# Projections by float32 matmuls on the two column halves of TensorE in place of three float32r passes

## The chip, the cores and the metric

The kernel runs on one core of a Trainium2 chip. The metric is the device time of one execution in microseconds (us). The runs shown are three, from 2896.31 to 2898.53 us with a median of 2897.43.

## The reference

The reference is one step of a two-layer streaming encoder with 1024 model features, for a prompt of 1024 frames and a group of 8 x 16 sample frames, 1152 frames in all. Everything is float32. Cut to its trunk:

```python
for i in range(DEPTH):                       # 2 layers
    a = _rms(h, norm_mix_pre[i])
    if i < N_A_LAYERS:                       # layer 0: forgetting attention, 16 heads x 64
        proj = a @ fox_w_in[i]               # q, k, v and the log-forget column
        ...
        mix = o.reshape(b, t, FOX_HEADS * HEAD_DIM) @ fox_w_out[i]
    else:                                    # layer 1: sliding window, 16 query and 4 key heads
        q = (a @ swa_w_q[j]).reshape(b, t, SWA_Q_HEADS, HEAD_DIM)
        o = swa_attend(q, kv_k, kv_v, swa_sinks[j])
        mix = o.reshape(b, t, SWA_Q_HEADS * HEAD_DIM) @ swa_w_out[j]
    h = h + _rms(mix, norm_mix_post[i])
    f = _swiglu(_rms(h, norm_ffn_pre[i]), ffn_w_gate[i], ffn_w_up[i], ffn_w_down[i])   # D_FF = 2816
    h = h + _rms(f, norm_ffn_post[i])
    gate = jax.nn.sigmoid(_rms(h, ple_norm[i]) @ ple_w_gate[i] + ple_b_gate[i])
    h = h + gate * (p[i] @ ple_w_proj[i])
    if i == N_A_LAYERS - 1:
        kv = (_rms(h, kv_norm) @ swa_w_kv).reshape(b, t, 2, SWA_KV_HEADS, HEAD_DIM)
```

The products written with `@` are the projections of the title. The attentions' own products (scores, weights times values) are not among them.

## The kernel before

Activations lie with features on the 128 partitions, in three chunks of C = 384 frames. A projection's weights are cut into blocks of 128 x 128; one output tile of 128 features by 384 frames collects eight such blocks (KT = 8) in one PSUM buffer, and ScalarE or VectorE takes it out.

**Parts.** Projections run in the matmul type float32r. Every operand of a projection is made into two tiles: a high part, `round_r` (line 139, a ScalarE copy into a float32r tile), and a low part, `low_part` (line 145, on VectorE: operand minus high part). The helper `mm3` (lines 215 to 217) then issues three float32r matmuls into the same PSUM tile: high weights by high activations, high by low, low by high. The value projections have the same three matmuls written out, with the activations as the stationary operand: `v_tile` of layer 0 (lines 578 to 580, 272 or 384 columns) and `v_tile` in `kv_steps` (lines 1859 to 1861, 256 columns).

**Where parts come from.** `Weights` loads raw weights (tile wraw), scales them where a norm's gain is folded in, and makes the tiles whi and wlo (`round`, `low`). Weights with the mark "parts" were split earlier: `presplit` loads a quarter of a unit, scales it, rounds it (line 1499), subtracts (line 1502), and stores both parts to wpg_d or wkq_d, in the shade of the channel mixer; `Weights.round` later loads both parts. Activations are split by `plan_split` (ahi, alo), `o_high`/`o_low`, `operand` (four high and four low slices of one tile), `c_high`/`c_low`, `p0_high`/`p0_low` and `ple_parts`.

**The channel mixer.** For two of the three chunks the gate, up and down projections use Strassen's scheme (seven products for a 2 x 2 cut of the weights and the chunks); the third chunk is multiplied plainly. `matrix` handles one pair of weight units of gate or up: sums of weights (`s_sum`, line 1314), their parts (`parts_of`), `product` (four mm3 into banks X, Y, Z) and `plain`. Results go to rows (tag row, 10 buffers) and to t_d and hc_d in device memory. The down projection is a loop of `kstep`: load one row of activations (`h_load`), split it (`h_high`, `h_low`), split the slice of weights (`w_high`, `w_low`), then 4 or 8 mm3 into PSUM tiles pd. `strassen` forms weight differences for it in two buffers of tag sq (`temp_diff`, line 1627) or in place (line 1632).

**Order.** In the first stage and in `layer_tail` the order of the instructions on each engine is made by `Plan`: each step is added with an engine, a cost in us, the steps it follows, the buffers it takes and frees and a due time; `run` simulates the four queues (PE, ACT, DVE, LOAD, the last being the load queue on SP) and emits the steps in the order found. `tile_steps` adds one projection tile in two or more pieces, `serpentine` runs a projection over the three chunks, turning round so that weights at the turn are used again. The two attentions are emitted in program order, with `Pipe` deciding when delayed work (transposes, values) comes in. In the second one `queries` (16 tiles in pieces of three, three and two blocks) and `embed` (24 tiles) are put between score rows by `fill`.

**float32 matmuls already there.** The attentions' values are such: `fox_values` (line 1007) and `swa_values` (line 2046) multiply, for two heads e = 0 and 1, 64 columns of values each, and write the two halves of the partitions of one PSUM tile, tile pV:

```python
for e in range(2):
    nc.tensor.matmul(pv[0][e * HD:(e + 1) * HD, q0:256], vp[:, j, e * HD:(e + 1) * HD],
                     PT[e][j // 4][:, j % 4, q0:], start=j == 0, stop=j == nj - 1)
```

So is the cumulative sum over frames (line 762, 16 columns of weights). Sums over features for the norms (`total`, line 233, three matmuls) and their spreading (`spread`, line 254, three transposes) are full-width PE work between the projection tiles.

Of the kernel before, what the change touches and what calls it, by code (L numbers as in the profile page):

```python
# [20 lines left out]
KT = 8  # L21
# [67 lines left out]
def tile_kernel(ctx: ExitStack, tc: tile.TileContext, i, o, upto=99):  # L89
# [53 lines left out]

    def low_part(out, x, hi):
        return nc.vector.tensor_tensor(out, x, hi.bitcast(F32), SUB)  # L145

    class Weights:
# [21 lines left out]
        def round(self, k):  # L169
            src, gain = self.specs[k]  # L170
            if gain == "parts":
                t = self.sets[k % len(self.sets)]
                hl = [wp.tile([P, 1024], F32R, name="w" + x, tag=f"w{x}{t}") for x in ("hi", "lo")]
                for x in range(2):
                    nc.sync.dma_start(hl[x].bitcast(F32), src[:, x])
                self.done[k] = hl
                return
# [8 lines left out]
            lo = wp.tile([P, 1024], F32R, name="wlo", tag=f"wlo{t}")  # L186
            self.done[k] = hi, lo
            return round_r(self.eng, hi[:, :n], raw[:, :n])

        def low(self, k):  # L190
            if k in self.raws:
                n = self.specs[k][0].shape[-1]
                hi, lo = self.done[k]
                return low_part(lo[:, :n], self.raws.pop(k)[:, :n], hi[:, :n])
# [17 lines left out]
    def mm3(ps, w, a, first, last, more=False):  # L212


        nc.tensor.matmul(ps, w[0], a[0], start=first, stop=False, skip_group_check=more)  # L215
        nc.tensor.matmul(ps, w[0], a[1], start=False, stop=False, skip_group_check=more)  # L216
        nc.tensor.matmul(ps, w[1], a[0], start=False, stop=last, skip_group_check=more)  # L217
# [111 lines left out]
    def plan_unit(plan, W, k, due=1e9, needs=()):  # L329
# [7 lines left out]
        if W.specs[k][1] == "parts":  # L337
            plan.turn[part] = [plan.add(LOAD, 2.9, step(W.load, k), turn(part), takes=[part])]
            return plan.turn[part][0]
# [8 lines left out]
        return plan.add(DVE, 0.07 + 0.00104 * n, step(W.low, k), [r], frees=["raw"])  # L348
# [42 lines left out]
    def plan_split(plan, src, after, put, free=(), read=()):  # L391
# [4 lines left out]
        def high(k):  # L396
            if not out:
                out.extend((act_slot(F32R, "ahi"), act_slot(F32R, "alo")))
                put(tuple(out))
            round_r("a", out[0][:, k, :], src()[:, k, :])  # L400

        def low(k):
            low_part(out[1][:, k, :], src()[:, k, :], out[0][:, k, :])

        for k in range(KT):
            x = plan.add(ACT, 0.42, step(high, k), [after[k]] + first, takes=[] if first else ["act", "act"])
            first = first or [x]
            done.append(plan.add(DVE, 0.47, step(low, k), [x] + done[-1:]))
        if free:
            plan.add(DVE, 0.0, lambda: None, done + list(read), frees=list(free))  # L410
# [49 lines left out]
    def w_out(l):  # L460
# [5 lines left out]
        keep(W.low(0))  # L466
        return W

    def out_parts(c, ks):
# [3 lines left out]
        def split(k):  # L473
            if not parts:
                parts.extend((act_slot(F32R, "ohi"), act_slot(F32R, "olo")))
            keep(round_r("a", parts[0][:, k, :], oc[c][:, k, :]))
            keep(low_part(parts[1][:, k, :], oc[c][:, k, :], parts[0][:, k, :]))
# [47 lines left out]
    def ple_parts(praw, c, part):  # L525

        pa = []
        for k in range(2):
            hi, lo = part(0), part(1)
            with tc.high_priority(offset=HP):  # L530
                round_r("a", hi, praw[:, c, k])
                low_part(lo, praw[:, c, k], hi)
# [36 lines left out]
    def v_tile(piece, blk, ps=None, ks=range(KT)):  # L569
# [5 lines left out]
        for k in ks:  # L575
            hi, lo = Wv.get(4 * piece + k // 2)
            ws = slice((k % 2) * n, (k % 2 + 1) * n)
            nc.tensor.matmul(ps[:, :n], ahi[:, k, ts], hi[:, ws], start=k == 0, stop=False)
            nc.tensor.matmul(ps[:, :n], ahi[:, k, ts], lo[:, ws], start=False, stop=False)
            nc.tensor.matmul(ps[:, :n], alo[:, k, ts], hi[:, ws], start=False, stop=k == KT - 1)  # L580
# [34 lines left out]
    def p0_high(c, k):  # L615
        hi, lo = (tp.tile([P, C], F32R, name="phl", tag=f"phl{x}", bufs=4) for x in range(2))
        round_r("a", hi, praw[:, c, k])
        pa.setdefault(c, []).append((hi, lo))

    def p0_low(c, k):  # L620
        low_part(pa[c][k][1], praw[:, c, k], pa[c][k][0])
# [16 lines left out]
    def wp_step(k, h, part):  # L638
# [6 lines left out]
        elif part == 1:  # L645
            if h == 0:
                Wp.done[k] = [wp.tile([P, 1024], F32R, name="w" + x, tag=f"w{x}{k}") for x in ("hi", "lo")]
            round_r("a", Wp.done[k][0][:, cs], Wp.raws[k][:, cs])
        else:
            low_part(Wp.done[k][1][:, cs], Wp.raws[k][:, cs], Wp.done[k][0][:, cs])  # L650
# [17 lines left out]
    for h in range(2):  # L668
        for k in range(2):
# [3 lines left out]
            wlow[h].append(plan.add(DVE, 0.6, step(wp_step, k, h, 2), [x], frees=["raw"] if h else []))  # L673
# [5 lines left out]

    def p0(c):  # L680
        split = []
        for k in range(2):
            x = plan.add(ACT, 0.42, step(p0_high, c, k), [px[c]], takes=["phl"])
            split.append(plan.add(DVE, 0.47, step(p0_low, c, k), [x], frees=["act"] if c == 2 and k else []))
        for f in range(KT):
            end = f == KT - 1
            x = plan.tile(0.985, step(p0_tile, c, f), split + wlow[f // 4], takes=["mm"],
                          frees=(["phl", "phl"] + (["w0", "w1"] if c == 2 else [])) if end else [])
            x = plan.add(ACT, 0.37, step(p0_out, c, f), [x], takes=["ev"] if c == 2 else [], frees=["mm"], due=plan.clock + EVAC)
# [12 lines left out]

    def v0(c):
# [4 lines left out]
        for blk in range(3 * c, 3 * c + 3):  # L708
            x = plan.tile(1.41, step(v0_tile, blk, 0), na[c][:4] + wv[:2], takes=["mm"])
            x = plan.tile(1.41, step(v0_tile, blk, 1), na[c][4:] + wv[2:] + [x], frees=["w0", "w1"] * 2 if blk == 8 else [])  # L710
# [353 lines left out]
    def layer_tail(l, oc, Wo, oa0, order, specs_kv=(), more=None):  # L1064
# [56 lines left out]
        def tile_steps(key, unit, act, needs_w, needs_a, frees=(), pieces=2):  # L1121
# [7 lines left out]
            for p in range(pieces):  # L1129
                x = plan.tile(4.17 / pieces, step(piece, p * n, n), [x] + needs_a[p * n:(p + 1) * n], takes=["mm"] if p == 0 else [],  # L1130
# [3 lines left out]
        def serpentine(W, at, order, act, needs, then, free):  # L1134
# [4 lines left out]
            last = {at[n][f]: (n, f) for n, f in seq}  # L1139
            for j, (n, f) in enumerate(seq):  # L1140
# [3 lines left out]
                               frees + (free if j % KT == KT - 1 else []), 2 if j % KT else NPC)  # L1144
# [3 lines left out]
        def o_high(c, k):  # L1148
            if oa[c] is None:
                oa[c] = act_slot(F32R, "ohi"), act_slot(F32R, "olo")  # L1150
            round_r("a", oa[c][0][:, k, :], oc[c][:, k, :])

        def o_low(c, k):
            low_part(oa[c][1][:, k, :], oc[c][:, k, :], oa[c][0][:, k, :])
# [3 lines left out]
        for c in order:  # L1158
            split, first = [], [None] * (c == cC)
            for k in range(KT):  # L1160
# [5 lines left out]
                split.append(plan.add(DVE, 0.47, step(o_low, c, k), [x] + split[-1:], frees=["act"] if k == KT - 1 else []))  # L1166
# [41 lines left out]
        def operand(name, c, k0, after=()):  # L1208

            def high(j):  # L1210
                if j == 0:
                    acts[name] = act_slot(F32R, name)
                round_r("a", acts[name][:, j], mix[c][:, k0 + j])

            def low(j):
                low_part(acts[name][:, 4 + j], mix[c][:, k0 + j], acts[name][:, j])

            for j in range(4):
# [3 lines left out]
                add(DVE, 0.47, step(low, j), r=[("m", c, k0 + j), (name, 0, j)], w=[(name, 1, j)])  # L1222
# [9 lines left out]
        def c_high(k):  # L1232
            if k == 0:
                cp_[:] = act_slot(F32R, "chi"), act_slot(F32R, "clo")
            round_r("a", cp_[0][:, k], mix[cC][:, k])

        def c_low(k):
            low_part(cp_[1][:, k], mix[cC][:, k], cp_[0][:, k])

        first = []  # L1240
        for k in range(KT):
            x = add(ACT, 0.42, step(c_high, k), r=[("m", cC, k)], w=[("chi", k)], after=first, takes=[] if k else ["act", "act"])
            first = first or [x]
            add(DVE, 0.47, step(c_low, k), r=[("m", cC, k), ("chi", k)], w=[("clo", k)])
# [15 lines left out]
        nC = [wrote["clo", k] for k in range(KT)]  # L1260
# [11 lines left out]
        def parts_of(m, u, src, skey):  # L1272
# [4 lines left out]
            def high():  # L1277
                units_[m, u] = [wp.tile([P, 1024], F32R, name="w" + x, tag=f"w{x}{t}") for x in ("hi", "lo")]
                round_r("a", units_[m, u][0], src())

            def low():
# [989 lines left out]
```

## Time and profile before

| what | value |
|---|---|
| median of three runs | 2897.43 us |
| the profiled execution | 2892.37 us, span 2890.6 us |
| TensorE (PE), matmuls | busy 2845.3 us, 98%, 17612 records |
| weight loads (PEld) | busy 2733.4 us, 95% |
| VectorE (DVE) | busy 1843.8 us, 64% |
| ScalarE (ACT) | busy 1259.9 us, 44% |
| GpSimd (POOL) | busy 198.3 us, 7% |
| data moved by DMA | 440.29 MB |

The stages by the lines at work: first projections to about 150 us, query and key projection of layer 0 to about 350, forgetting attention to 608, the tail of layer 0 (output projection, channel mixer, embedding gate, then the next layer's keys, values and first queries) to 1685, sliding-window attention to 1898, the tail of layer 1 to the end.

How to read a row of the groups: line, engine, operation, output<-input by tile names, then for matmuls rows*columns of the weights and partitions x elements of the moving operand, the number of records, busy time in us, mean ns of one, and the engine's idle time before them with what ended it. Both float32r and float32 are shown as f32. Matmul records overlap in a pipeline, so a mean is a latency. A row of the stretches gives for each engine busy us and records in brackets, then the granted clock of PE as a share of full speed, the DMA share and GB/s.

### The profile page before, as it was taken

The page shows a single profiled execution, that of the slowest core. Times are in us where ns is not written, and L with a number is a line of the kernel's source. Part 1 is how long each engine was busy: PE and PEld are TensorE (multiplying, and loading weights), DVE is VectorE, ACT ScalarE, POOL GpSimd, SP SyncE. Part 2 cuts the span into 40 slices and gives each one's busy share as a digit, 9 for nine tenths or more (in the row PEclk, how much of TensorE's full clock was granted, in tenths as well). Part 3 has the DMA queues.
Part 4 walks back from the last instruction along what each step waited for, and adds up shares of the span by engine and source line. Part 5 has one row for each costly group of instructions (what it writes and reads, how often), then busy time and mean ns, then how long its engine had stood idle before and what let it go on. Part 6 is the DMA issues. An engine that isn't in the chain of part 4 may idle for free. (4 is left out here: it accounts for less than half of the span.)

```text
span 2890.6 us, 47806 instructions
## 1 busy us (share of the span) xinstructions
PE 2845.3 (98%) x17612; PEld 2733.4 (95%) x17612; DVE 1843.8 (64%) x4139; ACT 1259.9 (44%) x2574; POOL 198.3 (7%) x324
## 2 busy tenths in 40 slices
PE   8999999999999999999999999999999999999999
PEld 8999977789999999999999988799999999999999
DVE  7254377767866656548888435658855555549884
ACT  6222266664433333335554245754433333335541
POOL 0000155510000000000000022300000000000000
PEclk9999999999999999999999999999999999999999
DMA  7364476624254545542365667433333333533364
GB/s 265 108 196 152 152 202 186 181 69 146 95 166 154 175 158 169 192 151 81 117 215 188 215 200 226 127 124 120 113 124 105 119 118 115 183 110 105 101 225 146
DMA packets 293215, 440.29 MB, mean 152 GB/s; under 512 B 38466, under 2 KB 246212, under 8 KB 292948
## 3 DMA queue, kind: packets, MB, share of 16 engines
q1 hardware_dynamic: 292980, 437.22, 47.5%
q8 instruction: 139, 2.28, 0.3%
q14 instruction: 96, 0.79, 0.1%
HBM read 302.75 MB, written 136.20 MB: 152 GB/s over the span
## 5 line engine op out<-in xcount | busy, mean ns | idle before, releaser
L215 PE MATMUL ps<-ahi,whi 128*128 128x384 f32 x1008 | 342.3, 340 | 0.7 <-ACT ev L588 0.7
L217 PE MATMUL ps<-ahi,wlo 128*128 128x384 f32 x1008 | 338.8, 336 | 0.4 <-DMA wlo<-wpg_d 0.4
L216 PE MATMUL ps<-alo,whi 128*128 128x384 f32 x1008 | 338.7, 336 | 0.0
L215 PE MATMUL pd<-row,whi 128*128 128x384 f32 x968 | 325.1, 336 | 3.1 <-ACT row L139 2.8
L216 PE MATMUL pd<-row,whi 128*128 128x384 f32 x968 | 323.8, 334 | 3.1 <-DVE row L145 3.1
L217 PE MATMUL pd<-row,wlo 128*128 128x384 f32 x968 | 323.5, 334 | 0.0
L215 PE MATMUL ps<-chi,whi 128*128 128x384 f32 x704 | 235.7, 335 | 0.0
L217 PE MATMUL ps<-chi,wlo 128*128 128x384 f32 x704 | 235.2, 334 | 0.0
L216 PE MATMUL ps<-clo,whi 128*128 128x384 f32 x704 | 235.2, 334 | 0.0
L145 DVE TENSOR_TENSOR wlo<-wraw,whi 128x1024 fp32r<-128x1024 f32 (+3 forms) x146 | 171.6, 1178 | 71.2 <-ACT whi L139 70.9
L139 ACT CAST whi<-wraw 128x1024 fp32r<-128x1024 f32 (+3 forms) x146 | 148.4, 1017 | 134.3 <-issue 42.1
L215 PEld LDWEIGHTS ps<-ahi,whi 128*128 128x128 f32 x1008 | 190.7, 189 | 6.2 <-issue 4.9
L217 PEld LDWEIGHTS ps<-ahi,wlo 128*128 128x128 f32 x1008 | 190.5, 189 | 0.8 <-DMA wlo<-wpg_d 0.7
L216 PEld LDWEIGHTS ps<-alo,whi 128*128 128x128 f32 x1008 | 190.7, 189 | 0.0
L215 PEld LDWEIGHTS pd<-row,whi 128*128 128x128 f32 x968 | 181.7, 188 | 5.1 <-ACT row L139 3.5
L216 PEld LDWEIGHTS pd<-row,whi 128*128 128x128 f32 x968 | 181.7, 188 | 3.8 <-DVE row L145 3.8
L145 DVE TENSOR_TENSOR wlo<-wd,whi 128x512 fp32r<-128x512 f32 (+1 forms) x154 | 129.2, 840 | 87.3 <-ACT whi L139 87.3
L139 ACT CAST whi<-wd 128x512 fp32r<-128x512 f32 (+1 forms) x154 | 114.6, 744 | 160.2 <-PE pd L216 137.9
L217 PEld LDWEIGHTS pd<-row,wlo 128*128 128x128 f32 x968 | 181.7, 188 | 0.0
L1350 ACT COPY row<-pX 128x384 f32<-128x384 f32 x120 | 57.8, 481 | 241.8 <-PE pX L217 234.3
L2018 POOL TENSOR_SCALAR tt<-tt,l 128x256 f32<-128x256 f32 (+1 forms) x128 | 59.9, 488 | 1230.1 <-PE ps L217 1105.9
L216 PEld LDWEIGHTS ps<-clo,whi 128*128 128x128 f32 x704 | 132.2, 188 | 0.0
(275 smaller groups left out, 7186.9 us busy)
## 6 DMA issues: line engine op xcount, KB each, us to landing
t_d<-row SPq DMA_DIRECT2D x154, 192.0 KB
row<-t_d SPq DMA_DIRECT2D x154, 192.0 KB
wraw<-in_w_gate SPq DMA_DIRECT2D x44, 512.0 KB
wraw<-in_w_up SPq DMA_DIRECT2D x44, 512.0 KB
wd<-in_w_down SPq DMA_DIRECT2D x44, 512.0 KB
wpg_d<-sq SPq DMA_DIRECT2D x64, 256.0 KB
st<-h_d SPq DMA_DIRECT2D x72, 192.0 KB
wraw<-in_w_out SPq DMA_DIRECT2D x24, 512.0 KB
```

Source lines behind the costliest of these rows:

```text
L139: return nc.scalar.copy(out, in_)
L145: return nc.vector.tensor_tensor(out, x, hi.bitcast(F32), SUB)
L215: nc.tensor.matmul(ps, w[0], a[0], start=first, stop=False, skip_group_check=more)
L216: nc.tensor.matmul(ps, w[0], a[1], start=False, stop=False, skip_group_check=more)
L217: nc.tensor.matmul(ps, w[1], a[0], start=False, stop=last, skip_group_check=more)
L1350: add(ACT, 0.37, lambda: nc.scalar.copy(put_row(temp(n)), ps(bank)), r=[(m, "ps", bank)], w=[(g, temp(n))], takes=["row"], **soon())
L2018: nc.gpsimd.tensor_scalar(tt[:, g, :nw], tt[:, g, :nw], l[:, g:g + 1], 1.0, op0=MULT, op1=MULT)
```

## The change

The low parts are gone. A new helper `whole` copies an operand on ScalarE with all its bits into the tile that held the high part, and mm3 issues two float32 matmuls, one for each 64 of the weight block's 128 columns, into partitions 0 to 63 and 64 to 127 of the same PSUM tile. The value projections call mm3 as well. `presplit` scales a quarter and stores it whole; loads of "parts" bring one tile. The down projection reads the loaded weights and rows directly, with no copy, and takes one row buffer a step. The costs given to `Plan` become 0.325 us for a product of 384 frames in place of 0.52, frees that hung on VectorE's subtraction move to ScalarE steps of no cost, and some PE steps name earlier PE steps that share a buffer. The attentions' own matmuls, and the splits of their queries and keys, stay.

```diff
+    def whole(out, in_):
+
+        return nc.scalar.copy(out.bitcast(F32), in_)
...
             if gain == "parts":
                 t = self.sets[k % len(self.sets)]
-                hl = [wp.tile([P, 1024], F32R, name="w" + x, tag=f"w{x}{t}") for x in ("hi", "lo")]
-                for x in range(2):
-                    nc.sync.dma_start(hl[x].bitcast(F32), src[:, x])
+                hl = [wp.tile([P, 1024], F32R, name="whi", tag=f"whi{t}")] * 2
+                nc.sync.dma_start(hl[0].bitcast(F32), src[:, 0])
...
-            self.done[k] = hi, lo
-            return round_r(self.eng, hi[:, :n], raw[:, :n])
+            self.done[k] = hi, hi
+            return whole(hi[:, :n], raw[:, :n])
...
     def mm3(ps, w, a, first, last, more=False):
 
 
-        nc.tensor.matmul(ps, w[0], a[0], start=first, stop=False, skip_group_check=more)
-        nc.tensor.matmul(ps, w[0], a[1], start=False, stop=False, skip_group_check=more)
-        nc.tensor.matmul(ps, w[1], a[0], start=False, stop=last, skip_group_check=more)
+        for e in (0, HD):
+            nc.tensor.matmul(ps[e:e + HD], w[0][:, e:e + HD].bitcast(F32), a[0].bitcast(F32), start=first, stop=last, skip_group_check=more)
...
         for k in range(KT):
             x = plan.add(ACT, 0.42, step(high, k), [after[k]] + first, takes=[] if first else ["act", "act"])
             first = first or [x]
-            done.append(plan.add(DVE, 0.47, step(low, k), [x] + done[-1:]))
+            done.append(x)
...
-            nc.tensor.matmul(ps[:, :n], ahi[:, k, ts], hi[:, ws], start=k == 0, stop=False)
-            nc.tensor.matmul(ps[:, :n], ahi[:, k, ts], lo[:, ws], start=False, stop=False)
-            nc.tensor.matmul(ps[:, :n], alo[:, k, ts], hi[:, ws], start=False, stop=k == KT - 1)
+            mm3(ps[:, :n], (ahi[:, k, ts],), (hi[:, ws],), k == 0, k == KT - 1)
...
-                x = plan.tile(4.17 / pieces, step(piece, p * n, n), [x] + needs_a[p * n:(p + 1) * n], takes=["mm"] if p == 0 else [],
+                x = plan.tile(2.6 / pieces, step(piece, p * n, n), [x] + needs_a[p * n:(p + 1) * n] + (list(end) if p == pieces - 1 else []), takes=["mm"] if p == 0 else [],
...
-            x = add(ACT, 0.95, high, r=skey, w=[(m, u, "hi")], after=plan.turn.get(f"w{t}", []), takes=[f"w{t}"])
+            x = add(ACT, 0.95, high, r=skey, w=[(m, u)], after=plan.turn.get(f"w{t}", []), takes=[f"w{t}"])
             plan.turn[f"w{t}"] = [x]
-            add(DVE, 1.13, low, r=[*skey, (m, u, "hi")], w=[(m, u)])
...
             def scale():
...
-                nc.vector.tensor_tensor(r3, r3, g_, MULT)
-
-            def high():
-                box["hl"] = tp.tile([P, 2, C], F32R, name="sq", tag="sq", bufs=NSQ)[:, :, :256]
-                nc.scalar.copy(box["hl"][:, 0], box["raw"])
-
-            def low():
-                nc.vector.tensor_tensor(box["hl"][:, 1], box["raw"], box["hl"][:, 0].bitcast(F32), SUB)
-                nc.sync.dma_start(dst[u][:, :, cs], box["hl"].bitcast(F32))
+                t = tp.tile([P, 2, C], F32, name="sq", tag="sq", bufs=NSQ)[:, 0, :256]
+                nc.vector.tensor_tensor(t.rearrange("p (k c) -> p k c", k=nk), r3, g_, MULT)
+                nc.sync.dma_start(dst[u][:, 0, cs], t)
...
             def h_load():
-                hp[s] = [None, row(F32R)]
-                nc.sync.dma_start(hp[s][1].bitcast(F32), hsrc)
-
-            def h_high():
-                hp[s][0] = row(F32R)
-                round_r("a", hp[s][0], hp[s][1].bitcast(F32))
-
-            def h_low():
-                low_part(hp[s][1], hp[s][1].bitcast(F32), hp[s][0])
...
+                hp[s] = [row()]
+                nc.sync.dma_start(hp[s][0], hsrc)
...
-                    mm3(tiles["D", d][:, :C], (parts_[s][0][:, ds_], parts_[s][1][:, ds_]), hp[s], new and start, stop, more=not new)
+                    mm3(tiles["D", d][:, :C], (wsrc()[:, ds_],), hp[s], new and start, stop, more=not new)
...
-                x = add(PE, 0.522 * len(ds), step(mms, ds), w=[("D", d) for d in ds], after=[h_done, w_done, x],
+                x = add(PE, 0.325 * len(ds), step(mms, ds), r=wkeys, w=[("D", d) for d in ds], after=[h_done, x],
                         takes=["mm" if ds[0] < 6 else "st"] if new and start else [],
-                        frees=["row", "row", f"w{t}"] if ds[-1] == seq[-1] else [])
+                        frees=["row"] if ds[-1] == seq[-1] else [])
```

More of the change, by code (lines that the diff above doesn't have):

```diff
@@ L337, in plan_unit @@
         if W.specs[k][1] == "parts":
-            plan.turn[part] = [plan.add(LOAD, 2.9, step(W.load, k), turn(part), takes=[part])]
+            plan.turn[part] = [plan.add(LOAD, 1.46, step(W.load, k), turn(part), takes=[part])]
             return plan.turn[part][0]
@@ L347, in plan_unit @@
         plan.turn["raw"], plan.turn[part] = [f], [r]
-        return plan.add(DVE, 0.07 + 0.00104 * n, step(W.low, k), [r], frees=["raw"])
+        return plan.add(ACT, 0.0, step(W.low, k), [r], frees=["raw"])
     def plan_rms(plan, src, after, out="rr", slot=None, ready=()):
@@ L615, in p0_high @@
     def p0_high(c, k):
-        hi, lo = (tp.tile([P, C], F32R, name="phl", tag=f"phl{x}", bufs=4) for x in range(2))
-        round_r("a", hi, praw[:, c, k])
+        hi = lo = tp.tile([P, C], F32R, name="phl", tag="phl0", bufs=4)
+        whole(hi, praw[:, c, k])
         pa.setdefault(c, []).append((hi, lo))
-    def p0_low(c, k):
-        low_part(pa[c][k][1], praw[:, c, k], pa[c][k][0])
     def p0_tile(c, f):
@@ L646, in wp_step @@
             if h == 0:
[L647 to L650, printed above, removed]
+                Wp.done[k] = [wp.tile([P, 1024], F32R, name="whi", tag=f"whi{k}")] * 2
+            whole(Wp.done[k][0][:, cs], Wp.raws[k][:, cs])
     def wp_loads(h):
```

121 lines of the change are left out of this document (49 added, 72 removed).

## The prediction

> **What bounds the kernel now.** I read three views of the profile in this order: its first part (busy time of each engine), the forty slices, and then the busy time in chosen stretches, one inside the channel mixer (2100 to 2400 us) and one in the second layer's attention (1700 to 1900 us).
>
> ```profile
> span 2890.6 us, 47806 instructions
> PE 2845.3 (98%) x17612; PEld 2733.4 (95%) x17612; DVE 1843.8 (64%) x4139; ACT 1259.9 (44%) x2574; POOL 198.3 (7%) x324
> ...
> PE   8999999999999999999999999999999999999999
> ...
> PEclk9999999999999999999999999999999999999999
> ```
>
> ```profile
> core 0: us, PE busy (x) PEld busy (x) DVE busy (x) ACT busy (x) POOL busy (x), PEclk, DMA share, GB/s
> 2100.00:2400.00 300.00, 300.00 (x1733) 300.00 (x1732) 164.37 (x258) 98.89 (x154) 0.00 (x0) 1.00 0.35 117
> 1700.00:1900.00 200.00, 196.72 (x1237) 165.22 (x1236) 126.38 (x510) 131.95 (x457) 56.57 (x120) 1.00 0.62 183
> ```
>
> TensorE (PE) is busy for 2845.3 of 2890.6 us, in every slice but the first at nine tenths or more, and at the full granted clock throughout. In the stretch of the channel mixer it is busy all 300.00 us; VectorE is at 164.37 and ScalarE at 98.89 of 300. Even in the attention stretch PE has only 200 - 196.72 = 3.3 us free. So what is taken off VectorE, ScalarE or the DMA queues is hidden beside PE and worth at most PE's 45.3 us of idle time in the whole span; what an edit does to PE's own stream is on the path that sets the end, nearly one for one. The forecast is therefore a count of projection products multiplied by the price of one, before and after.
>
> The count. The helper mm3 issues three matmuls (lines 215, 216, 217) for each product of one 128x128 weight block with 128x384 activations. One row per operand of line 215 counts the products; line 578 does the same for the value projection, whose blocks are 384 or 272 wide:
>
> ```profile
> L215 PE MATMUL ps<-ahi,whi 128*128 128x384 f32 x1008 | 342.3, 340 | 0.7 <-ACT ev L588 0.7
> L215 PE MATMUL pd<-row,whi 128*128 128x384 f32 x968 | 325.1, 336 | 3.1 <-ACT row L139 2.8
> L215 PE MATMUL ps<-chi,whi 128*128 128x384 f32 x704 | 235.7, 335 | 0.0
> L215 PE MATMUL ps<-ohi,whi 128*128 128x384 f32 x384 | 129.6, 337 | 0.0
> L215 PE MATMUL pX<-T,whi 128*128 128x384 f32 x320 | 107.1, 335 | 2.2 <-ACT whi L139 2.2
> L215 PE MATMUL pX<-Y,whi 128*128 128x384 f32 x320 | 106.9, 334 | 0.0
> L215 PE MATMUL pY<-T,whi 128*128 128x384 f32 x320 | 106.9, 334 | 0.0
> L578 PE MATMUL ps<-whi,ahi 128*128 128x384 f32 x144 | 48.2, 335 | 0.0
> L215 PE MATMUL pZ<-Y,whi 128*128 128x384 f32 x160 | 53.4, 334 | 0.0
> L215 PE MATMUL ps<-Y,whi 128*128 128x384 f32 x128 | 43.1, 337 | 0.0
> L215 PE MATMUL ps<-phl,whi 128*128 128x384 f32 x96 | 35.1, 365 | 8.5 <-ACT phl L139 8.5
> ```
>
> 1008 + 968 + 704 + 384 + 320 + 320 + 320 + 160 + 128 + 96 = 4408 products by mm3, and 144 of line 578 with 384 columns: 4552. The price of one today comes from the stretch 2100 to 2400, which holds nothing but these: 300.00 us / 1733 records = 0.1731 us a matmul, so three are 0.519 us. (The 334 to 340 ns means in the rows are latencies of pipelined instructions, not the spacing.) 4552 x 0.519 = 2364 us, 82% of the span.
>
> **The change, part by part.**
>
> **1. The price of a product on PE.** The new mm3 issues two float32 matmuls, each with 64 of the 128 weight columns, to the two halves of the PSUM rows. The kernel already has float32 matmuls, so the trace before shows what they cost. The cumulative sum of line 762 is one, 16 columns wide; the last row is a float32r matmul of 256 columns:
>
> ```profile
> L762 PE MATMUL ps<-tri,lf 128*16 128x384 f32 x4 | 1.6, 486 | 0.0
> L762 PE MATMUL ps<-tri,lf 128*16 128x256 f32 x4 | 1.2, 379 | 0.0
> L762 PE MATMUL ps<-tri,lf 128*16 128x128 f32 x4 | 0.8, 272 | 0.0
> L1859 PE MATMUL ps<-whi,ahi 128*128 128x256 f32 x72 | 20.4, 283 | 0.0
> ```
>
> The page has x4 where the program has two instructions of each width: a float32 matmul is two records, so two passes. The duration grows by 486 - 379 = 107 ns per 128 columns, 0.836 ns a column; with 384 columns one pass streams for 321 ns and two for 642 ns, however few weight columns it uses. The float32r rows go from 283 ns at 256 columns to 334 at 384 (line 215 above), 51 ns per 128. A float32 pass therefore streams at half the speed of a float32r matmul, and there are two of them: four times the streaming time of one float32r matmul.
>
> Do the two halves run side by side? Exactly this form, two 64-column float32 matmuls on the two halves, one behind the other, is in both attentions (lines 1007 and 2046, tile pV). The timeline, merged, with start, time, and the next instruction's start:
>
> ```profile
> 563.05 2.60 PE L1007 MATMUL pV<-PT,aux 128*64 128x256 f32 x24
> 565.58 0.33 PE L984 MATMUL pT<-ident,tt 128*128 128x128 f32 x1
> ```
> ```profile
> 1877.26 1.94 PE L2046 MATMUL pV<-PT,Vs 128*64 128x512 f32 x8
> 1879.13 0.62 PE L2003 MATMUL S<-K,QR 128*128 128x256 f32 x3
> ```
>
> The first group is 24 records: two halves, two passes, five pieces of 256 columns and one of 128 (at the diagonal block), 1408 columns of half pairs, from 563.05 to 565.58: 2.53 us. The second is 8 records, two pieces of 512, 1024 columns, 1877.26 to 1879.13: 1.87 us. One after the other, four passes of 512 columns would need 4 x 512 x 0.836 ns = 1.71 us a piece, 3.42 us for two; 1.87 us was measured, so the halves do overlap completely. The two groups differ by 384 columns and 0.66 us: that is directly one new product. The rest, 1.87 - 1024 x 0.66/384 = 0.11 us, is the change of the array's layout. The two ways give 0.642 us (slope) and 0.66 (difference of rounded starts); I take 0.645, next to the slope, since that comes from four records of equal length and leaves 1.5 ns a pass for issue.
>
> Weight loads don't add: a 64-column load takes
>
> ```profile
> L1007 PEld LDWEIGHTS pV<-PT,aux x640: 132/137/137, 365.1 to 607.4; 128*64 128x64 f32 x160
> ```
>
> 137 ns at the median, and in the first group above two of them fit into each slot of 214 ns; the new product has two per 321 ns.
>
> So a product goes from 0.519 to 0.645 us: +0.126 x 4552 = +572 us. The halves overlap each other, but a full-width matmul filled both halves already; splitting doubles the number of instructions and overlapping them gives that back, no more. Three single passes became the time of four.
>
> **2. The value projections** with 272 and 256 columns, 72 products each:
>
> ```profile
> L578 PE MATMUL ps<-whi,ahi 128*128 128x272 f32 x72 | 20.8, 289 | 0.0
> 1660.00:1683.00 23.00, 23.00 (x194) 23.00 (x193) 0.76 (x2) 4.61 (x11) 0.00 (x0) 1.00 0.39 119
> ```
>
> 23.00 us / 194 = 0.119 us a matmul, 0.356 for three; new 0.645 x 256/384 = 0.430: +0.074 x 72 = 5.3 us, and 272/256 of that for the other 72, 5.7. Together +11 us.
>
> **3. New changes of layout.** Between full-width work and halves the array pays, by the 0.11 us above. Projections today are full width like the statistics and score matmuls around them; afterwards every full-width instruction inside a projection stage is a change to and fro. Row sums and their spreading are
>
> ```profile
> L233 PE MATMUL pstat<-ones,acc 128*128 128x1 f32 x180 | 23.2, 244 | 11.9 <-DVE acc L365 11.9
> L254 PE MATMUL prms<-ident,ry 128*128 128x128 f32 x90 | 14.7, 272 | 0.0
> ```
>
> 180 / 6 = 30 and 90 / 3 = 30 groups. In the second attention the query projection comes in 16 tiles of 3 pieces, the embedding in 24 tiles, each between full-width score matmuls: 72. That is 132 round trips. The 0.11 covers one side for certain; 132 x 0.11 = 15 us and, if both sides pay, 29. I take +25, nearer the upper end since the view shows the start of the group only after the first delay.
>
> **4. Work taken from other engines.** VectorE loses the low parts and ScalarE the rounding of the down projection's operands (kstep):
>
> ```profile
> L145 DVE TENSOR_TENSOR wlo<-wraw,whi 128x1024 fp32r<-128x1024 f32 (+3 forms) x146 | 171.6, 1178 | 71.2 <-ACT whi L139 70.9
> L145 DVE TENSOR_TENSOR wlo<-wd,whi 128x512 fp32r<-128x512 f32 (+1 forms) x154 | 129.2, 840 | 87.3 <-ACT whi L139 87.3
> L1627 DVE TENSOR_TENSOR sq<-wd 128x512 f32<-128x512 f32 x44 | 30.2, 686 | 10.0 <-DMA wd<-in_w_down 9.7
> L139 ACT CAST row<-row 128x384 fp32r<-128x384 f32 x198 | 99.9, 510 | 53.9 <-DMA row<-hc_d 39.9 <-DVE wlo L145 8.0 <-PE pd L216 4.1
> ```
>
> The activations and gate/up weights keep a ScalarE copy (whole). The down projection now reads the loaded weights and rows as they are; presplit loses its rounding and its subtraction, its store and the later load halve. All this lies beside PE; it is worth only what PE waits for today:
>
> ```profile
> PE pstat L233 <- DVE acc L365: 11.9, 8, 2.8
> PE ps L215 <- ACT phl L139: 8.5, 2, 8.0
> PE pd L216 <- DVE row L145: 3.1, 3, 1.5
> ```
>
> 8.0 us of the phl row is the first load and stays, as does the end of the program, some 5 us. That leaves 45.3 - 13 = 32 us of waits within; a slower PE with lighter neighbours should lose most of them: -20, bounds 0 and -32. What comes late next is nothing but PE itself.
>
> **5. Waits that are new.** Down weights and differences (temps, two buffers of tag sq) are now read by PE, so VectorE's next difference waits for PE instead of ScalarE. A difference takes 0.69 us (30.2 / 44), PE has 4 x 0.645 = 2.6 us of the other buffer to work on: covered; uncovered it would be 44 x 0.69 = 30 us. Behind it on VectorE stand only the additions of finished down tiles. On the load queue the row load keeps its place and loses one buffer; presplit's store now waits for the scaling alone and the stores behind it come earlier. The emission order is made with 0.325 us a product, half of what I expect; PE then reaches each step later than the order assumes, so its operands are there; ScalarE's copies into weight buffers, though, wait for PE with evictions queued behind them, about 1 us each time. I cost that at nothing, hidden by six PSUM tiles, and up to +40 if the cover fails in places.
>
> **Sum:** 572 + 11 + 25 - 20 = +588 on the profiled execution's 2892.4 us (span 2890.6): 3480. The median of the runs shown is 5 above that execution, so 3485 us.
>
> **The rivals.**
> *Two halves give a factor of two (faster).* If the two 64-column matmuls together took half of 0.645, 0.3225 us, the sum would be -0.197 x 4552 = -897, about -19 for the narrower ones, +25 - 20: 1980 us. For it: the halves overlap, and the emission order is written with 0.325. Against it: the pV rows already contain that overlap, and still give 0.66 us per 384 columns of both halves. It would decide from 0.519 us a product downwards, 1.35 ns a column against 1.72 measured. The Trainium skill, TensorEngine Tiling (Array Packing), section Theoretical Speedup, gives "up to 2x" for a dimension of at most 64; that speaks for small operands packed side by side, and by it, applied here, the time would be this 1980; the pV rows disagree when the operand was 128 wide to begin with. Chance 4%. That the halves stay single-pass float32r despite the new type would end lower still, near 1320 us by two overlapped matmuls of 0.173 us; 1%.
> *The halves run one after the other (far slower).* In pV each half streams its own activations, here both stream the same tile; no row shows that. If this kept them apart, a product costs 2 x 0.645 = 1.29 us: 2892 + 0.77 x 4552 = about 6400 us. Chance 3%.
> *The price is right, but the order fails.* If buffers freed late by a slower PE leave ScalarE and VectorE blocked in order, a wait of 1 to 2 us in most of the 44 gate and up passes and in some of the 198 down steps comes on top: 3600 to 3750 us. For it: evictions wait in order behind weight copies. Against: VectorE loses at least the 171.6 + 129.2 us of its two rows above, so it is below half load. Chance 5%.
>
> **How the numbers follow.** The likeliest case has 87%: 3485, its own range 3440 (0.642, no layout price, all waits gone) to 3580 (0.66 a product, +82 - 14). Low 3435, high 3600 leaves out the far rivals and most of the third. Within 0.2% (6 us, what a measurement here can tell from no change) there is almost nothing: 1%. Faster 5%, slower 94%.
>
> **What would show it.** Matmul records: 4 for each of 4696 products, 18784, for 14088 now, so 22300 in all; in a stretch of the mixer 300 us should hold about 1860 of them, two starting together every 0.32 us. PE at 98 to 99% of a span of some 3480; VectorE down by more than those 301 us. Wrong would be: four records in 0.32 us (first rival), in 1.29 (second), or PE idle over 100 us (third).

## The result, and the profile after

The changed kernel takes 3498.43 us (median of 4 runs, 3498.11 to 3503.94) against 2896.87 us for the kernel before: 1.208 times as long, 95% interval 1.2059 to 1.2101. The profiled execution took 3498.51 us, its span is 3496.7.

The first part of the profile after and the slices:

```profile
span 3496.7 us, 55029 instructions
PE 3451.6 (99%) x22308; PEld 1692.2 (48%) x22308; DVE 1205.7 (34%) x3169; ACT 989.3 (28%) x2066; POOL 195.7 (6%) x324
...
PE   8999999998999999999999999998999999999999
...
PEclk9999999999999999999999999999999999999999
```

TensorE (PE) has 22308 records, where about 22300 were counted ahead, and is busy for 99% of the longer span. VectorE has fallen from 1843.8 to 1205.7 us, ScalarE from 1259.9 to 989.3, and the end has moved the other way. The stretch that answers to 2100 to 2400 us of before lies in the second layer's mixer:

```profile
core 0: us, PE busy (x) PEld busy (x) DVE busy (x) ACT busy (x) POOL busy (x), PEclk, DMA share, GB/s
2500.00:2800.00 300.00, 300.00 (x1864) 133.62 (x1861) 80.30 (x151) 74.44 (x111) 0.00 (x0) 1.00 0.28 94
```

300.00 us / 1864 records x 4 = 0.644 us a product, before 0.519. PE's weight loads, busy all the time before, now fill 133.62 of 300 us. The groups, with 64 columns of weights and four records for one product (4032 = 4 x 1008), are

```profile
L215 PE MATMUL ps<-a,whi 128*64 128x384 f32 x4032 | 662.5, 487 | 2.8 <-DVE row L1636 2.1
L215 PE MATMUL pd<-row,wd 128*64 128x384 f32 x3168 | 517.6, 486 | 0.0
L215 PE MATMUL ps<-c,whi 128*64 128x384 f32 x2816 | 477.2, 491 | 19.1 <-ACT c L146 19.1
```

and PE's waits, with total, times and longest:

```profile
PE ps L215 <- ACT c L146: 19.1, 4, 8.7
PE ps L215 <- ACT phl L146: 8.2, 1, 8.2
PE prms L252 <- DVE ry L245: 5.0, 2, 2.5
```

The waits for low parts (PE pd, row L145) are gone and new ones have come: 19.1 us for operand c (the chunk that is multiplied plainly), nearly all of it in two waits of about 9 us, and 5.0 us for the spreading of a norm. The 8.2 us for phl are the first load, which was there before.

### The profile page after: what moved, and what is told of

Same layout as the page of the kernel before. It is cut to its first block, busy times and chain, and to the rows that moved or that the text cites. A ratio compares the mean times of both kernels' runs of the same rounds, so it can differ in the third digit from the quotient of the medians.

```text
span 3496.7 us, 55029 instructions
## 1 busy us (share of the span) xinstructions
PE 3451.6 (99%) x22308; PEld 1692.2 (48%) x22308; DVE 1205.7 (34%) x3169; ACT 989.3 (28%) x2066; POOL 195.7 (6%) x324
## 4 chain that ended last, share of the span: by engine, by line
PE 98%; DVE 1%; ACT 0%; issue 0%; DMA 0%; POOL 0%; SPq 0%; POOLq 0%; DVEq 0%; ACTq 0%
PE ps L215 48%; PE pd L215 18%; PE pX L215 12%; PE pY L215 6%; PE pZ L215 3%; PE S L957 2%; PE pT L976 2%; PE pV L999 2%; PE S L1957 1%; PE pT L1977 1%; PE pV L2000 1%; PE pstat L231 1%; PE prms L252 0%; PE po L819 0%; PE sV L878 0%
## 5 line engine op out<-in xcount | busy, mean ns | idle before, releaser
L215 PE MATMUL ps<-a,whi 128*64 128x384 f32 x4032 | 662.5, 487 | 2.8 <-DVE row L1636 2.1
L215 PE MATMUL pd<-row,wd 128*64 128x384 f32 x3168 | 517.6, 486 | 0.0
L215 PE MATMUL ps<-c,whi 128*64 128x384 f32 x2816 | 477.2, 491 | 19.1 <-ACT c L146 19.1
L215 PEld LDWEIGHTS ps<-a,whi 128*64 128x64 f32 x4032 | 285.5, 137 | 355.0 <-issue 347.4
L215 PEld LDWEIGHTS pd<-row,wd 128*64 128x64 f32 x3168 | 225.8, 137 | 280.7 <-issue 266.8
L215 PEld LDWEIGHTS ps<-c,whi 128*64 128x64 f32 x2816 | 202.0, 138 | 274.3 <-issue 250.2
L215 PE MATMUL ps<-o,whi 128*64 128x384 f32 x1536 | 251.6, 487 | 0.0
L215 PE MATMUL pX<-Y,whi 128*64 128x384 f32 x1280 | 223.5, 492 | 0.0
L215 PE MATMUL pX<-T,whi 128*64 128x384 f32 x1280 | 220.0, 486 | 0.0
L215 PE MATMUL pY<-T,whi 128*64 128x384 f32 x1280 | 220.0, 486 | 0.0
```

What stands on the lines that cost most here:

```text
L215: nc.tensor.matmul(ps[e:e + HD], w[0][:, e:e + HD].bitcast(F32), a[0].bitcast(F32), start=first, stop=last, skip_group_check=more)
```

## Experiments

The kernel before, run beside these experiments, has a median of 2899.55 us, and of 2902.44 beside the quarters, half by half and GpSimd; the ratios are against those.

**Full width.** One float32 matmul of all 128 columns in place of the two halves:

```diff
-        for e in (0, HD):
-            nc.tensor.matmul(ps[e:e + HD], w[0][:, e:e + HD].bitcast(F32), a[0].bitcast(F32), start=first, ...)
+        nc.tensor.matmul(ps, w[0].bitcast(F32), a[0].bitcast(F32), start=first, stop=last, skip_group_check=more)
```

> The changed kernel with one float32 matmul of all 128 columns for each product in place of two halves; order and everything else as it is. Theory (two passes at half the speed, however many columns of the array take part): the product stays at 0.645 us, 644 to 650 by the trace, and only the changes of layout go, so 3498 becomes about 3474 (24 us less, 15 to 29). Rival (splitting bought time, a full-width float32 pass streams slower or waits for its 128-column weight load): slower than 3498, 6400 if a full-width product takes the time of two halves in a row. Rival (the waits are the cause): 3498 unchanged.

Measured: 3473.47 us, 1.1972 of before (1.1947 to 1.1998). The same stretch of the mixer:

```profile
2500.00:2800.00 300.00, 300.00 (x932) 176.78 (x931) 81.61 (x154) 72.02 (x106) 0.00 (x0) 1.00 0.27 87
```

Two records a product, 300.00 / 932 x 2 = 0.644 us: the halves buy nothing on PE, and about 25 us of the changed kernel are the price of going to and fro between layouts. (3498.43 - 3473.47 = 25; PE's busy time falls from 3451.6 to 3423.7, by 28, at the same mean clock of 0.995.) The timelines show where the price falls. Here are the three sums of a norm between two projection tiles, in the changed kernel and at full width:

```profile
799.90 0.83 PE L231 MATMUL pstat<-ones,acc 128*128 128x1 f32 x6
800.66 7.96 PE L215 MATMUL ps<-o,whi 128*64 128x384 f32 x48
```
```profile
795.70 0.72 PE L230 MATMUL pstat<-ones,acc 128*128 128x1 f32 x6
796.28 7.99 PE L214 MATMUL ps<-o,whi 128*128 128x384 f32 x24
```

From the start of the sums to the next projection it is 800.66 - 799.90 = 0.76 us among halves and 796.28 - 795.70 = 0.58 among full widths.

**Quarters.** One size changed, four matmuls of 32 columns a product:

```diff
-        for e in (0, HD):
-            nc.tensor.matmul(ps[e:e + HD], w[0][:, e:e + HD]...
+        for e in range(0, P, 32):
+            nc.tensor.matmul(ps[e:e + 32], w[0][:, e:e + 32]...
```

> The changed kernel with four matmuls of 32 columns a product on the four quarters in place of two halves: one size changed. Theory (a pass has the same time whatever its width, and all groups overlap): 0.645 us a product as before, 3490 to 3530, with twice the matmul records. Rival (narrower matmuls are cheaper, the factor that splitting was meant to bring): 2000 to 2900. Rival (the eight weight loads and starts of a product become the limit): 3600 and more, eight loads of 0.1 us in a row would be 0.8 us a product.

Measured: 3497.5 us in one run.

```profile
2500.00:2800.00 300.00, 300.00 (x3728) 120.97 (x3724) 80.35 (x151) 73.16 (x109) 0.00 (x0) 1.00 0.30 96
```

3728 records, eight a product: 0.644 us again. Full width, halves and quarters give one number: a pass over 384 columns of activations takes 0.322 us whatever the number of weight columns, and narrower ones fill the same time side by side. The whole kernel has 41092 records in place of 22308 and takes no longer, so the 25 us above are not a price of the number of instructions.

**True costs for the planner.** The halves stay, the costs given to `Plan` are doubled:

```diff
-                x = plan.tile(2.6 / pieces, step(piece, p * n, n), ...
+                x = plan.tile(5.16 / pieces, step(piece, p * n, n), ...
...
-                x = add(PE, 0.325 * len(ds), step(mms, ds), ...
+                x = add(PE, 0.645 * len(ds), step(mms, ds), ...
```

(likewise 0.65 to 1.3, 0.95 to 1.84, 1.3 to 2.58 and 1.74 to 3.45).

> The changed kernel, halves kept, with the planner's costs of the projections doubled to what the trace shows (0.645 us for a product of 384 frames, 0.46 for 272, 0.43 for 256). Theory: the price is untouched, 0.645 us a product; the waits of PE on the third chunk's operands at the start of each channel mixer (19.1 us in all) and on the spreading of the norms (5.0 us) come from an order made for a PE twice as fast and go, 3498 becomes 3470 to 3485. Rival (the order is the main cause of the rise): 3300 or less. Rival (those waits are a plain dependence on the norm's chain, whatever the order): 3498.

Measured: 3473.04 us, 1.197 of before (1.194 to 1.2). PE's longest waits now:

```profile
PE ps L215 <- ACT phl L146: 8.7, 1, 8.7
PE pstat L231 <- DVE acc L363: 6.7, 4, 2.7
PE pstat L231 <- DVE lf L581: 2.7, 1, 2.7
```

The wait for c and the one for the spreading are gone; 6.7 us for the sum of a norm have come back. The timeline of the changed kernel shows what the order did at the first mixer (start, time, engine, line, tile; the wait in brackets), and the waits from 828 to 845 us what ScalarE waited for:

```profile
816.81 7.91 PE L215 MATMUL ps<-c,whi 128*64 128x384 f32 x48
825.41 5.38 PE L215 MATMUL ps<-c,whi 128*64 128x384 f32 x32
831.20 1.51 PE L215 MATMUL ps<-c,whi 128*64 128x384 f32 x8
841.28 1.55 PE L215 MATMUL ps<-c,whi 128*64 128x384 f32 x4 [8.58 <-ACT c L146]
```
```profile
ACT c L146 <- DVE mix L1189: 8.8, 2, 8.2
```

Through 48 + 32 + 8 records, 22 products, PE worked on c, then stood for 8.58 us until ScalarE could copy another slice of it, and ScalarE waited up to 8.2 us for VectorE's scaling of that slice by the norm (line 1189). The norm of c was not late: VectorE's timeline shows six of its eight slices scaled by it before 804.7 us, and the seventh only at 840.07:

```profile
803.01 1.67 DVE L1189 SCALAR_TENSOR_TENSOR mix<-mix,gains,rr 128x384 f32<-128x384 f32 x3
831.82 1.15 DVE L418 SCALAR_TENSOR_TENSOR y<-y,gains,rr 128x384 f32<-128x384 f32 x2 [1.56 <-ACT rr L376]
840.07 0.61 DVE L1189 SCALAR_TENSOR_TENSOR mix<-mix,gains,rr 128x384 f32<-128x384 f32 x1
```

In between, in VectorE's order, stand the operations that finish another chunk (lines 418, 422 and 363), fifteen of them from 831.82 us on alone. They had to wait for that chunk's norm, and its sums and their spreading lie in PE's order between the products on c. So PE held up VectorE, and VectorE, working in order, held up PE. With true costs all eight slices are scaled in one go, long before PE comes to c at 829.72 us, and the products on it run through. The scalings of c in the changed kernel, the same with true costs, and PE's timeline with true costs:

```profile
L1189 DVE SCALAR_TENSOR_TENSOR mix<-mix,gains,rr x8: 610/611/618, 795.2 to 842.6; 128x384 f32<-128x384 f32 x8
```
```profile
L1189 DVE SCALAR_TENSOR_TENSOR mix<-mix,gains,rr x8: 609/610/620, 769.5 to 773.2; 128x384 f32<-128x384 f32 x8
```
```profile
829.72 5.33 PE L215 MATMUL ps<-c,whi 128*64 128x384 f32 x32
835.74 5.38 PE L215 MATMUL ps<-c,whi 128*64 128x384 f32 x32
841.52 10.54 PE L215 MATMUL ps<-c,whi 128*64 128x384 f32 x64
```

That the order is the cause is shown by this; why the planner's reckoning parted the scalings was not traced. And the wait costs more than itself. Two stretches, the wait and what follows, with the granted clock in the third column from the end:

```profile
832.00:837.00 5.00, 0.71 (x6) 0.04 (x2) 5.00 (x11) 0.52 (x1) 0.00 (x0) 0.99 0.66 192
837.00:850.00 13.00, 7.78 (x26) 3.32 (x28) 10.92 (x30) 5.91 (x8) 0.00 (x0) 0.50 0.55 178
```

From 837 to 850 us the clock is 0.50. The Trainium skill, TensorE: Matmul & The Clock Gate, section HAM oscillation — how this bites in real kernels, gives the rule that no gap of PE should be longer than about 3.4 us, since the clock is halved in a longer one and the work behind it starts cold. The trace agrees for this wait of 8.58 us, and again for one of 8.65 us in the second layer, with the clock at half from 2414 us. But shorter waits did it too. In the kernel before, PE waits 2.85 us for the sum of a norm, and the clock is at half behind it although PE is busy throughout:

```profile
1516.89 1.41 PE L233 MATMUL pstat<-ones,acc 128*128 128x1 f32 x6 [2.85 <-DVE acc L365]
1517.00:1523.00 6.00, 6.00 (x21) 6.00 (x22) 5.62 (x21) 2.97 (x6) 0.00 (x0) 0.50 0.34 100
```

The measurement decides: 3.4 us is not the least wait that halves the clock here. As to the price, of the 13 us at half clock in the changed kernel the first 4.3 are still the wait, and PE is busy for 7.78; at full clock that work would have taken half as long, so the estimate is some 4 us on top of the 8.58.

**Both.**

> Both edits: full-width float32 matmuls and the planner's costs at 0.645 us a product. Theory: the two gains add, about 3450 (3440 to 3465); still slower than before by some 550 us, the difference of 0.645 and 0.519 us on 4552 products less what remains of the waits. Rival (layout and waits are the same time counted twice): as the better of the two alone.

Measured: 3454.12 us, 1.1902 of before (1.1875 to 1.1929). The two gains, 25 and 25 us, give 44 together, and part of the missing 6 is the clock: at a mean clock of 0.999 the runs with true costs span 3470.2 to 3471.1 us and this kernel 3446.5, which is 24 less. The granted clock and span of the changed kernel and of this one:

```profile
core 0: 3496.7 us, clock 0.995
```
```profile
core 0: 3446.5 us, clock 0.999
```

This is the shortest version with float32 projections, and the price of the product keeps it 555 us above before.

**Relief alone.** The kernel before with its order, all three matmuls on the high parts, no low parts made, stored or loaded, so that its results are not those of the kernel before:

```diff
-        nc.tensor.matmul(ps, w[0], a[1], start=False, stop=False, skip_group_check=more)
-        nc.tensor.matmul(ps, w[1], a[0], start=False, stop=last, skip_group_check=more)
+        nc.tensor.matmul(ps, w[0], a[0], start=False, stop=False, skip_group_check=more)
+        nc.tensor.matmul(ps, w[0], a[0], start=False, stop=last, skip_group_check=more)
...
-                low_part(units_[m, u][1], src(), units_[m, u][0])
+                proj_low(units_[m, u][1], src(), units_[m, u][0])      # returns None
```

> The kernel before with its order and its three float32r matmuls a product, but VectorE computes no low parts for projections, none are stored or loaded, and all three matmuls take the high parts, so the low terms of the products are left out. It is the relief of the other engines without the new price on PE. Theory (that work lies beside PE): 2897 less at most the 32 us of PE waits inside the span, I expect 10 to 20: 2877 to 2887. Rival (the load on VectorE and the DMA queues holds PE back more than its waits show): below 2860.

Measured: 2863.03 us, 0.987 of before (0.9849 to 0.9891), 36.5 us less than the 2899.55 of the runs beside it: more than I expected and somewhat over the bound of 32, but short of the rival's 2860. Page and clock:

```profile
span 2861.4 us, 46256 instructions
PE 2836.9 (99%) x17612; PEld 2730.3 (95%) x17612; DVE 1213.7 (42%) x3169; ACT 1245.8 (44%) x2574; POOL 195.3 (7%) x324
```
```profile
core 0: 2861.4 us, clock 1.000
```
```profile
core 0: 2890.6 us, clock 0.998
```

(the last row is before). PE's idle time falls from 45.3 to 2861.4 - 2836.9 = 24.5 us, 21 less, and its busy time by 8.4 us with the same 17612 records. By the mean clocks, 0.998 and 1.000, some 6 of these 8.4 are the clock (an estimate, 0.002 x 2890); the rest is not assigned. The two profiles are 29.2 us apart and the medians 36.5, since the runs of before beside this one had mean clocks of 0.994 to 0.997, lower than the profiled 0.998. The bound left out that a wait also slows the work behind it.

**Half by half.** In `feat` the loop over the halves goes outside the loop over the blocks:

```diff
-        for k in ks:
-            mm3(ps, (hi[:, k, :], lo[:, k, :]), (a[0][:, k, :], a[1][:, k, :]), ...
+        for e in (0, HD):
+            for k in ks:
+                nc.tensor.matmul(ps[e:e + HD], hi[:, k, e:e + HD].bitcast(F32), a[0][:, k, :].bitcast(F32), ...
```

> The changed kernel, but in the helper that multiplies a whole tile (feat) the loop over the halves is outside: all blocks of features 0 to 63 first, then those of 64 to 127, so that neighbours in the stream use the same half. This touches about 2000 of the 4552 products. Theory (each half streams a pass in 0.322 us and only neighbours on different halves overlap): a product costs up to 1.29 us there, 15 of 16 passes no longer overlap within a tile in two pieces somewhat less: 3498 becomes 4600 to 4800. Rival (PE takes passes out of order and finds the other half's work, or each half alone streams at full speed): 3498 to 3600.

Measured: 3719.07 us in one run, between the two ranges. The query and key projection of layer 0, where eight blocks of one half follow one another, here and in the changed kernel:

```profile
200.00:500.00 300.00, 300.00 (x1226) 138.49 (x1223) 53.95 (x85) 31.68 (x62) 8.19 (x8) 1.00 0.29 95
```
```profile
200.00:400.00 200.00, 200.00 (x1242) 89.14 (x1240) 52.91 (x86) 31.70 (x62) 8.58 (x8) 1.00 0.43 143
```

300.00 / 1226 x 4 = 0.979 us a product against 200.00 / 1242 x 4 = 0.644. Had nothing overlapped it would be 1.29; had order not mattered, 0.644. A tile of eight blocks is 32 passes of 0.322 us and took 8 x 0.979 = 7.83 us, 24.3 passes long; so 7.7 passes of a tile ran beside one of the other half, about four at each of its two changes of half. The next half's work begins when some four passes of this one, two instructions, are not yet done. The Trainium skill, TensorE: Matmul & The Clock Gate, section The mechanism, has matmuls start and end strictly in program order; by that one pass, or the two passes of one instruction, could overlap at a change, 30 or 28 passes or 9.66 or 9.02 us a tile. The measurement decides: the start is not in the order of the program as written, within two instructions. In tiles cut into pieces of four blocks most of the loss is gone. The output projection of layer 0 is cut so:

```profile
829.66 54.77 PE L223 MATMUL ps<-o,whi 128*64 128x384 f32 x322
```

It takes (884.36 - 829.66) / 322 x 4 = 0.68 us a product (884.36 is the start of what follows), which is why the whole kernel lost only 221 us.

**Low parts on GpSimd.** An attempt at a faster kernel with all parts kept, after the gain by relief:

```diff
-            low_part(out[1][:, k, :], src()[:, k, :], out[0][:, k, :])
+            (nc.gpsimd if "row" in plan.free else nc.vector).tensor_tensor(out[1][:, k, :], src()[:, k, :], ...
...
-                nc.vector.tensor_tensor(box["hl"][:, 1], box["raw"], ...
+                nc.gpsimd.tensor_tensor(box["hl"][:, 1], box["raw"], ...
```

> The kernel before, results unchanged, with two of VectorE's subtractions on GpSimd: the low parts of the gate's and the next layer's activations and those of presplit, some 83 us of VectorE's time near the norms. The look at relief alone gave 1.3%; this keeps all parts. Theory (PE's waits and the half clock after them come from VectorE's chain at the norms): 2 to 15 us faster, 2882 to 2898. Rival (GpSimd is slower than VectorE here, and PE then waits for its low parts at the start of the gate): 5 to 40 us slower.

Measured: 2935.4 us, 1.0112 of before (1.0095 to 1.0129): about 1% slower, clear of the noise, in the rival's range. The two groups on GpSimd, the same on VectorE before, and PE's longest wait:

```profile
L1502 POOL TENSOR_TENSOR sq<-st,sq 128x256 fp32r<-128x256 f32 x112 | 125.8, 1135 | 1078.6 <-ACT sq L1499 1003.4 <-DMA t_d<-row 75.2
L403 POOL TENSOR_TENSOR alo<-y,ahi 128x384 fp32r<-128x384 f32 x72 | 89.1, 1256 | 676.4 <-ACT ahi L139 414.5 <-DVE wlo L145 261.7
```
```profile
L1502 DVE TENSOR_TENSOR sq<-st,sq 128x256 fp32r<-128x256 f32 x112 | 43.7, 420 | 10.7 <-ACT sq L1499 10.5
L145 DVE TENSOR_TENSOR alo<-y,ahi 128x384 fp32r<-128x384 f32 x72 | 39.4, 553 | 3.6 <-ACT ahi L139 3.5
```
```profile
PE pstat L233 <- DVE acc L365: 23.0, 11, 4.6
```

GpSimd takes 1135 and 1256 ns where VectorE took 420 and 553, and PE's wait for the norms' sums grows from 11.9 to 23.0 us. That the rival named: GpSimd is slower. But PE does not wait for the low parts themselves; it waits for VectorE's sums, and VectorE has become slower where GpSimd subtracts. GpSimd and VectorE side by side:

```profile
1478.76 8.10 POOL L403 TENSOR_TENSOR alo<-y,ahi 128x384 fp32r<-128x384 f32 x6 [261.72 <-DVE wlo L145]
```
```profile
1480.91 1.37 DVE L145 TENSOR_TENSOR row<-row 128x384 fp32r<-128x384 f32 x1
```

This subtraction on VectorE (row<-row) took 553 ns in the mean before and takes 1.37 us here. VectorE's additions for the norms (line 365), at most 560 ns before, take up to 1367. In the whole span PE is idle for 2938.0 - 2869.2 = 68.8 us, 23.5 more than before, and busy for 23.9 us more with the same records, at a mean clock of 0.991. What slows VectorE there was not tested. No version tried beats the kernel before with its results.

## Why the prediction was right, point by point

1. *Price of a product.* 0.645 us forecast, 0.644 measured, 0.125 x 4552 = +569 us of the 601.6. The value matmuls of the attentions had held the whole answer: slope and difference of two groups. The slope (0.642) came nearer than the difference of the two starts (0.66).
2. *Value projections.* +11 us forecast, not measured apart by a run.
3. *Layout.* +25 forecast, 25 measured by full width under the old order, 3473.04 - 3454.12 = 19 under the true costs, 24 there at equal clock. The count of 132 round trips was not checked; the total agrees.
4. *Waits of PE: -20 forecast, wrong in both its parts.* Relief by itself is worth 36.5 us, not 20, since the clock comes back with the waits (the forecast read the clock in tenths, as full throughout; its mean was 0.998 in the profile and 0.994 to 0.997 in the runs beside the experiment); and PE's idle time did not fall at all (45.3 before, 45.1 after).
5. *New waits: cost at nothing, up to 40 if the cover fails.* They cost 25 us by true costs under halves, 3473.47 - 3454.12 = 19 at full width. The step that failed is the sentence that PE reaches each step late, so that its operands are there. A slower PE comes late, but what it waits for comes late with it: the sums and spreadings of the norms are PE's own work, VectorE waits for them, and the scaling of c stands behind that in VectorE's order. ScalarE's copies into weight buffers and the differences of the down projection did not show up as waits.

The two errors of 4 and 5 partly cancelled. 569 + 11 + 25 - 36.5 + 25 = 594 of 601.6 us; some 8 us are assigned by no run. That the measured time lies within 14 us of the forecast 3485 owes something to this: with the layout and the price right, the two terms on waits were off by 16.5 and 25 us in opposite directions. The ends of the range do not follow from the terms named for them: 0.642, no layout and all waits gone gives 3485 - 14 - 25 - 12 = 3434, not 3440, and 0.66 a product gives 3485 + 68 = 3553, not 3580. Full-width float32 with true costs leaves a like gap: 569 + 11 - 36.5 = 544 against 555.

The rivals: the factor of two is refuted by three widths at one price (the pV rows, with 64 columns of weights for each head, had shown what two halves cost, and only full width shows that a 128-wide block gains nothing by them); halves one after the other are refuted by 0.644 with one moving tile for both. The third, that a slower PE leaves VectorE blocked in its order, named the right kind of trouble, at 25 us instead of 115 and more; what came late was a norm and not a freed buffer. Only the 2.1 us for VectorE's row of line 1636, which takes a finished tile out, look like the latter.

## What to carry to other kernels

Before splitting a full-width operation to run its parts side by side, multiply the parts' time by their number over the lanes: what was full already cannot gain, and the price of the new form may already stand in the trace on another line, to be had from two groups that differ only in size. Where instruction order comes from a cost model, a cost that is wrong by two leaves waits of its own even when the engine is slower than the model says. A wait of TensorE of several microseconds is to be counted with the half clock behind it. Work moved to another engine is not free for the engine it leaves: its remaining operations may take longer beside it.

## What the runs showed of the hardware that was not expected

- In a wait of 8.58 us the granted clock fell to 0.50 and stayed there for 13 us, 7.78 of them busy, which costs some 4 us more (an estimate); behind a wait of 2.85 us in the kernel before it was at half too.
- Weight width does not enter a float32 product's time at all: 128, 64 and 32 columns give 0.644 us, with 2, 4 and 8 records and as many weight loads.
- float32 matmuls on one half start before earlier ones in the program on the other half have started, but only about four passes ahead: 0.979 us a product with eight blocks in a row on a half, between 0.644 and 1.29.
- A subtraction of 128x384 float32 took 1256 ns on GpSimd and 553 on VectorE, and while GpSimd subtracted, one on VectorE took 1.37 us.
